# Layer 1 of a two-layer backbone: the output projection of the first eight heads beside the last head, for both halves of the columns

## The chip, the cores and the metric

The kernel runs on one core of one Trainium2 chip. The metric is the time of one execution on the device, in microseconds. Beside it there is one execution recorded by the hardware profiler, with its trace; that execution's own time stands in the table below.

Engines: PE multiplies matrices, PEld is its weight load, ACT, DVE and POOL work on SBUF and PSUM (the matmul accumulators), SP issues loads and POOL issues stores as DMA transfers. Each engine runs its instructions in the order of the built program; a waiting instruction holds all later ones of its engine.

## The reference, cut to what matters

The program computes two layers over 1024 latent tokens of width 1024 and 256 context tokens. Layer 1, the odd one, is a bidirectional gated linear recurrence of 16 heads, each with 128 value columns. What the change touches is its end, the product with `w_out`, the gate and the residual:

```python
def merge(o, z):
    o = _rms(jnp.swapaxes(o, 1, 2).astype(z.dtype), h_norm.reshape(HG_HEADS, HG_VDIM))
    return (o.reshape(o.shape[:2] + (HG_VW,)) * jax.nn.silu(z)) @ w_out
...
x = x + gate * y_lat
```

So out[1024, 1024] = x1 + gate * (y[1024, 2048] @ w_out[2048, 1024]), with y the normed and gated output of the 16 heads, 128 columns from each.

## The kernel before, in words

Everything is float32. For the matrix engine each operand is split in two parts, high and low: `split` (L72) casts the high part on ACT (L74) and subtracts it on DVE to get the low part (L75). A product then takes three matmuls for each block of 128 rows of the contraction: in `out_sum` yh by wh (L749), yh by wl (L750), yl by wh (L751), each 128 x 512.

Layer 1 is a loop over the 16 heads (`for h in range(16)`, in `build`). For each head: projections of the next head, scores inside chunks (`hg_intra`, the products named s and acc), the scan over states (`hg_scan`), then the norm and gate (squares on ACT at L1204 into gss, further steps on POOL and DVE, gz at L1208), and `hg_y`, which transposes gz on PE (tr, L1220), copies it (L1222, gyt) and stores the head's y by POOL's queue (L1223) to the DRAM array yd2 (printed yd) in two halves of 256 KB. The program is written in this order, but the tile framework's scheduler places each engine's instructions by priority and by when their inputs are there, so that matmuls of a later stage can stand between those of the last head.

The output projection is cut into 8 row tiles (tt, 128 tokens each), two halves of the columns (b = 1: columns 512 to 1023; b = 0: columns 0 to 511) and two halves of the contraction (q = 0: heads 0 to 7; q = 1: heads 8 to 15). One row tile for one b and one q is 8 blocks by 3 = 24 matmuls into one PSUM tile (mm). For it `out_y` (L730) reads y back from DRAM by SP (L736) in two halves of 256 KB into the raw buffers "wraw" of pool yp (3 of them), and splits each into yh and yl (2 buffers each). The weights for one b and q are 8 slabs of 128 x 512 (256 KB), loaded by SP (L103) into raw buffers and split into pairs of slab buffers (`wblock`, L80; its argument `ring` says for each slab which pool and how many buffers).

The stages before:

1. `out_ahead`, beside the last head (pool yp is opened when the normed input, hh and hl, is no longer needed, after the last projection, whose result gvT is copied at L1048): slabs of b = 1, q = 0 into a ring of 8 in yp ("wo"), raw in the heads' pool; 8 row tiles, each copied by ACT (L771) to SBUF (oacc). Then the slabs of b = 1, q = 1: four in pool wp ("w"), four in yp, raw in yp "woraw", 4 buffers.
2. Pool op1, b = 1: per row tile the product with q = 1, the row block of x1 (L782, oxh), then on DVE the addition of oacc (L786), the product with the gate (L788, og), the addition to x1 (L789), and the store of the result by POOL's queue (L1466). After each row tile two slabs of w1 are loaded and split: w1 holds all 16 slabs of b = 0 (`wo_half`, L726), with the four raw buffers "woraw".
3. b = 0: per row tile the product over q = 0 and q = 1 together (48 matmuls), no addition, gate and residual as above.

## Time and profile before

| | before |
|---|---|
| median of 3 runs | 3529.34 us (3528.73 to 3532.45) |
| the profiled execution's own time | 3531.36 us |
| its span in the trace | 3529.6 us |
| mean granted PE clock | 0.993 |
| PE busy | 3462.1 us, 24438 matmuls |

How to read it: the span runs from the first to the last instruction in the trace; the execution's own time is 1.8 us longer. PE is busy in 98% of the span. In the rows below, a line such as L749 is one of the kernel before; `mm<-woh,yh` means that mm is written from woh and yh, and an engine's idle time is put down to what released it last.

### The profile page before, as it was taken

The numbers are of one execution on the slowest core, as the hardware profiler recorded it, in microseconds if no ns is written. First come the engines' busy times: TensorE is split into PE (matmuls) and PEld (weight loads), VectorE is DVE, ScalarE is ACT, GpSimd is POOL, SyncE is SP. The second block draws the span as 40 slices with busy tenths as digits, with TensorE's granted clock in tenths as the row PEclk, the third lists the DMA queues.
The fourth block names the chain that finished last, engine by engine and source line by source line (L and its number), as shares of the span: only waits on it lengthen the run. The fifth ranks groups of instructions, "written<-read, shape, count | busy, mean of one in ns | idle before, by whom it ended". The sixth has DMA issues, their size and how long they took to land.

```text
span 3529.6 us, 64866 instructions
## 1 busy us (share of the span) xinstructions
PE 3462.1 (98%) x24438; PEld 3151.1 (89%) x24438; DVE 2370.4 (67%) x6001; ACT 1598.3 (45%) x3692; POOL 521.4 (15%) x836
## 2 busy tenths in 40 slices
PE   8999999999999999999999999999999999999988
PEld 5899999999999999987778999899999999999877
DVE  4669856766666654666677766577777777777852
ACT  5532135555444534555547323344444444444431
POOL 3211121222222211211211111001000000100010
PEclk9999999999999999999999999999999999999999
DMA  7542321322323225455483232212112111211353
GB/s 235 175 156 84 122 87 52 94 84 74 82 73 90 74 87 162 140 168 157 131 251 124 99 111 85 87 40 62 50 49 61 60 47 53 62 50 48 108 188 114
DMA packets 372618, 359.71 MB, mean 102 GB/s; under 512 B 30041, under 2 KB 322841, under 8 KB 372177
## 3 DMA queue, kind: packets, MB, share of 16 engines
q1 hardware_dynamic: 328944, 248.25, 23.9%
q0 software_dynamic: 43360, 107.32, 9.0%
q8 instruction: 193, 3.16, 0.4%
q14 instruction: 121, 0.98, 0.1%
HBM read 274.00 MB, written 81.32 MB: 101 GB/s over the span
## 4 chain that ended last, share of the span: by engine, by line
PE 83%; issue 8%; DMA 3%; DVE 2%; ACT 2%; POOL 1%; SPq 0%; POOLq 0%; DVEq 0%; ACTq 0%
PE mm L129 15%; PE mm L128 15%; PE mm L127 15%; PE s L1134 6%; PE acc L695 3%; PE tr L675 2%; PE sa L128 2%; PE sa L127 2%; PE sa L129 2%; PE acc L478 2%; PE s L485 2%; PE s L1179 1%; PE mm L749 1%; PE mm L750 1%; PE mm L751 1%
## 5 line engine op out<-in xcount | busy, mean ns | idle before, releaser
L127 PE MATMUL mm<-wh,hh 128*128 128x256 f32 x2256 | 648.8, 288 | 3.8 <-DVE ev L938 2.7
L128 PE MATMUL mm<-wl,hh 128*128 128x256 f32 x2256 | 648.8, 288 | 2.0 <-DVE wl L75 1.9
L129 PE MATMUL mm<-wh,hl 128*128 128x256 f32 x2256 | 648.4, 288 | 0.0
L129 PE MATMUL mm<-hh,wl 128*128 128x512 f32 (+1 forms) x1344 | 491.4, 366 | 0.0
L127 PE MATMUL mm<-hh,wh 128*128 128x512 f32 (+1 forms) x1344 | 485.2, 361 | 0.0
L128 PE MATMUL mm<-hl,wh 128*128 128x512 f32 (+1 forms) x1344 | 483.7, 360 | 0.0
L127 PEld LDWEIGHTS mm<-wh,hh 128*128 128x128 f32 x2256 | 431.1, 191 | 11.8 <-issue 6.9
L128 PEld LDWEIGHTS mm<-wl,hh 128*128 128x128 f32 x2256 | 431.4, 191 | 7.3 <-DVE wl L75 2.8
L129 PEld LDWEIGHTS mm<-wh,hl 128*128 128x128 f32 x2256 | 431.0, 191 | 3.6 <-issue 0.7
L74 ACT CAST wh<-wraw 128x512 fp32r<-128x512 f32 x282 | 173.4, 620 | 256.3 <-PE mm L128 125.7
L128 PEld LDWEIGHTS mm<-hl,wh 128*128 128x128 f32 x1344 | 254.0, 189 | 32.0
L129 PEld LDWEIGHTS mm<-hh,wl 128*128 128x128 f32 x1344 | 253.9, 189 | 30.5 <-issue 0.2
L127 PEld LDWEIGHTS mm<-hh,wh 128*128 128x128 f32 x1344 | 254.3, 189 | 29.3
L1125 ACT COPY gksel<-gK 128x512 f32<-128x512 f32 x224 | 147.0, 663 | 213.5 <-PE s L1134 204.4
L75 DVE TENSOR_TENSOR wl<-wraw,wh 128x512 fp32r<-128x512 f32 x282 | 191.2, 686 | 53.8 <-ACT wh L74 51.2
L1134 PE MATMUL s<-gQ,gksel 128*128 128x128 f32 x1536 | 199.8, 276 | 0.0
L1134 PEld LDWEIGHTS s<-gQ,gksel 128*128 128x128 f32 x1536 | 192.4, 191 | 7.0
L749 PE MATMUL mm<-woh,yh 128*128 128x512 f32 x444 | 180.4, 407 | 6.8 <-ACT yh L74 4.1
L751 PE MATMUL mm<-woh,yl 128*128 128x512 f32 x444 | 178.7, 403 | 0.7 <-DVE yl L75 0.5
L750 PE MATMUL mm<-wol,yh 128*128 128x512 f32 x444 | 177.8, 400 | 0.0
L1155 DVE TENSOR_TENSOR gQ<-gQ,gT 128x256 f32<-128x256 f32 x384 | 143.2, 414 | 28.1 <-PE s L1134 28.1
L74 ACT CAST wh<-b 128x512 fp32r<-128x512 f32 x124 | 77.0, 622 | 187.8 <-PE sa L129 79.5
(461 smaller groups left out, 8456.9 us busy)
## 6 DMA issues: line engine op xcount, KB each, us to landing
wraw<-yd SPq DMA_DIRECT2D x144, 256.0 KB
wraw<-in_wc_dram SPq DMA_DIRECT2D x128, 256.0 KB
wraw<-in_wab_dram SPq DMA_DIRECT2D x98, 256.0 KB
md<-ev POOLq DMA_DIRECT2D x94, 256.0 KB, 2.8
adar<-in_wada_dram POOLq DMA_DIRECT2D x32, 512.0 KB, 5.0
b<-in_wc_dram SPq DMA_DIRECT2D x64, 256.0 KB
vzd<-qo POOLq DMA_DIRECT2D x56, 256.0 KB, 2.5
adar<-in_wada_dram SPq DMA_DIRECT2D x16, 512.0 KB
```

What stands on the lines that cost most here:

```text
L74: nc.scalar.copy(hi, x)
L75: nc.vector.tensor_tensor(out=lo, in0=x, in1=hi.bitcast(F32), op=ALU.subtract)
L127: mm(ps, lhsT=lh(k), rhs=rh(k), start=(first and k == 0), stop=False)
L128: mm(ps, lhsT=lh(k), rhs=rl(k), start=False, stop=False)
L129: mm(ps, lhsT=ll(k), rhs=rh(k), start=False, stop=(last and k == nk - 1))
L695: m = nc.tensor.matmul(yp[h64], lhsT=v[:, h64], rhs=pTs[hd][:nk, i, :], start=(i == turn[0]), stop=(i == turn[-1]), tile_position=(0, hd * ...
L749: mm(ps, lhsT=yh[:, k, :], rhs=w.h(kk), start=(kk == 0), stop=False)
L750: mm(ps, lhsT=yh[:, k, :], rhs=w.l(kk), start=False, stop=False)
L751: mm(ps, lhsT=yl[:, k, :], rhs=w.h(kk), start=False, stop=(kk == 8 * len(qs) - 1))
L1125: nc.scalar.copy(ksel.rearrange("p (b s i) -> p b s i", s=2, i=h), pick(K))
L1134: nc.tensor.matmul(pa[:, c, :].rearrange("p (b s i) -> p b s i", s=2, i=h), lhsT=ksel[:, c * P : (c + 1) * P], rhs=qp[:, c * nbc : (c + 1) ...
L1155: nc.vector.tensor_tensor(out=t[:, i, :, s, :], in0=t[:, i, :, s, :], in1=bc(tot), op=ALU.mult)
```

## The change

Both halves of the columns are now computed for heads 0 to 7 (q = 0) beside the last head. The function `out_some`, which layer 0 uses already, does it: first for b = 1, with the sum kept in SBUF (oacc) as before, then for b = 0, where ACT copies the sum to a buffer ("ox", 2 of them) and POOL's queue stores it to a new DRAM array, `part`. For b = 0 the last stage then multiplies only q = 1 (24 matmuls a row tile), reads the part back by SP into a buffer of the op "og" (now 4 buffers, shared with the gate product) and adds it on DVE.

The slabs of the three blocks beside the last head (b = 1 q = 0, b = 0 q = 0, b = 1 q = 1) go through one list of 12 places: four in pool wp, eight in yp. The first block takes wp's four first, then yp; the third block takes only yp's eight. All three use the heads' pool for raws (3 buffers). The later slabs w1 are now 8 (b = 0, q = 1), in a pool of their own, and their raw buffers are yp's "wraw", 3 of them, the same that y is read into; two slabs are loaded after each of the first four row tiles of b = 1.

```diff
--- before.py
+++ after.py
@@ -723,10 +723,6 @@
         nc.gpsimd.dma_start(out=self.yd[p2], in_=z)
 
 
-    def wo_half(self, wsrc, rings, raw, later):
-        return self.wblock(None, "wo", [wsrc[:, 0:512]], 16, 512, raw, later=later, ring=rings)
-
-
     def out_y(self, tt, q, ysrc, yp, bufs, rp=None):
         yh = self.t(yp, [P, 8, P], F32R, "yh", bufs)
         yl = self.t(yp, [P, 8, P], F32R, "yl", bufs)
@@ -752,26 +748,14 @@
 
 
 
-    def out_some(self, w, q, order, ysrc, yp, acc):
+    def out_some(self, w, q, order, ysrc, yp, acc, dst):
         for tt in order:
             ps = self.ps("mm", [P, 512])
             self.out_sum(ps, w, tt, (q,), ysrc, yp, 2)
             o = self.t(yp, [P, 512], F32, "ox", 2) if acc is None else acc[:, tt, :]
             self.nc.scalar.copy(o, ps)
             if acc is None:
-                self.nc.gpsimd.dma_start(out=self.x1[tt * P : (tt + 1) * P, 0:512], in_=o)
-
-    def out_ahead(self, wsrc, nt, ysrc, yp, ring, rp=None):
-        acc = self.t(yp, [P, nt, 512], F32, "oacc", 1)
-        rows = lambda q: [wsrc[q * D : (q + 1) * D, 512:D]]
-        w = self.wblock(yp, "wo", rows(0), 8, 512, *((rp, 3, "wraw") if rp else (yp, 4, "woraw")), ring=ring)
-        for tt in range(nt):
-            ps = self.ps("mm", [P, 512])
-            self.out_sum(ps, w, tt, (0,), ysrc, yp, 2)
-            self.nc.scalar.copy(acc[:, tt, :], ps)
-        n = self.slabs if rp else 0
-        rings = [(self.wp, "w", n)] * n + [(yp, "wo", ring)] * (8 - n)
-        return acc, self.wblock(yp, "wo", rows(1), 8, 512, yp, 4, "woraw", ring=rings)
+                self.nc.gpsimd.dma_start(out=dst[tt * P : (tt + 1) * P, 0:512], in_=o)
 
 
     def out_tile(self, w, b, tt, ysrc, xsrc, xt, yp, op, bufs, ys=None, part=None):
@@ -1242,6 +1226,7 @@
             self.vzd = self.scratch(dr, "vzd", [2, LAT, 2 * D])
             self.md_all = self.scratch(dr, "md", [20, T, 256])
             self.md = {}
+            self.part = self.scratch(dr, "part", [LAT, 512])
 
             self.ident = self.t(cp, [P, P], F32, "ident")
             make_identity(nc, self.ident)
@@ -1363,7 +1348,7 @@
                             if g == ML_OUT[b][0]:
                                 wq[b] = wo(0, b)
                             for tt in [t for t, at_g in zip(ML_ORDER, ML_OUT[b]) if at_g == g]:
-                                self.out_some(wq[b], 0, [tt], self.yd, yp, acc if b else None)
+                                self.out_some(wq[b], 0, [tt], self.yd, yp, acc if b else None, self.x1)
                 w2 = wo(1, 1)
                 self.gate_bc(0, yp, 2, 1)
                 for tt in [8, 9, 3, 4, 2, 5, 1, 6, 0, 7]:
@@ -1449,20 +1434,30 @@
 
                 rh.close()
                 yp = es.enter_context(tc.tile_pool(name="oy", bufs=1, side="right"))
-                acc, w2 = self.out_ahead(a["woc"], 8, self.yd2, yp, 8, self.rawp)
-            self.ogb = 1
+                acc = self.t(yp, [P, 8, 512], F32, "oacc", 1)
+                ring = [(self.wp, "w", 4)] * 4 + [(yp, "wo", 8)] * 8
+                wo = lambda q, b, ring, raw, later=None: self.wblock(
+                    None, "wo", [a["woc"][q * D : (q + 1) * D, b * 512 : b * 512 + 512]], 8, 512, raw, later=later, ring=ring
+                )
+                raw = [pool, 3, "wraw"]
+                for i, b in enumerate((1, 0)):
+                    w = wo(0, b, (ring * 2)[8 * i : 8 * i + 8], raw)
+                    self.out_some(w, 0, range(8), self.yd2, yp, acc if b else None, self.part)
+                w2 = wo(1, 1, ring[4:], raw)
+            self.ogb = 4
             with tc.tile_pool(name="op1", bufs=2) as op, ExitStack() as wl:
                 later = []
                 wl1 = wl.enter_context(tc.tile_pool(name="wo1", bufs=1))
-                w1 = self.wo_half(a["woc"], [(wl1, "wo", 16)] * 16, [yp, 4, "woraw"], later)
+                w1 = wo(1, 0, [(wl1, "wo", 8)] * 8, [yp, 3, "wraw"], later)
                 for b, w in ((1, w2), (0, w1)):
                     self.gate_bc(1, op, 1, b)
                     for tt in range(8):
                         xt = self.t(op, [P, 512], F32, "oxh", 3)
-                        self.out_tile(
-                            w, b, tt, self.yd2, self.x1[tt * P : (tt + 1) * P], xt, yp, op, 2,
-                            part=acc[:, tt, :] if b else None,
-                        )
+                        part = acc[:, tt, :]
+                        if not b:
+                            part = self.t(op, [P, 512], F32, "og", 4)
+                            dma(out=part, in_=self.part[tt * P : (tt + 1) * P, :])
+                        self.out_tile(w, b, tt, self.yd2, self.x1[tt * P : (tt + 1) * P], xt, yp, op, 2, part=part)
                         nc.gpsimd.dma_start(out=a["out"][tt * P : (tt + 1) * P, b * 512 : (b + 1) * 512], in_=xt)
                         for ld in later[:2]:
                             ld()
```

Lines behind L764 of before have a number smaller by 16 in the changed kernel (L749 to L751 are L745 to L747, L736 is L732, L1208 is L1192, L1220 is L1204); the copies of L771 are at L756.

The scheduler decides the order on each engine. On PE, the end of the last head stood like this before (acc and tr belong to the last head, mm to the output projection of heads 8 to 15; numbers tell buffers apart):

```order
L1195 MATMUL acc_39323<-gv_39083,gA_38792 128x128
L1196 MATMUL acc_39323<-gS_7782_39256,gQ_38789 128x128
L1220 MATMUL tr_39360<-ident_73,gz_39085 128x128
L1197 MATMUL acc_39323<-gS_7810_39336,gQ_38789 128x128
L1195 MATMUL acc_39323<-gv_39083,gA_38792 128x128
L1196 MATMUL acc_39323<-gSc_7702_38932,gQ_38789 128x128
L1197 MATMUL acc_39323<-gS_7812_39343,gQ_38789 128x128
L1220 MATMUL tr_39368<-ident_73,gz_39085 128x128 x4
L749 MATMUL mm_39777<-woh_39742,yh_39778 128x512
```

and the same second half of the last head's transposes now, with the sums of b = 0, heads 0 to 7 (mm_39956 is the sixth row tile, mm_39994 the seventh):

```order
L746 MATMUL mm_39956<-wl_39754,yh_39957 128x512
L747 MATMUL mm_39956<-wh_39755,yl_39958 128x512
L1204 MATMUL tr_39369<-ident_74,gz_39086 128x128 x3
L745 MATMUL mm_39956<-wh_39761,yh_39957 128x512
L1204 MATMUL tr_39369<-ident_74,gz_39086 128x128
L746 MATMUL mm_39956<-wl_39760,yh_39957 128x512
L747 MATMUL mm_39956<-wh_39761,yl_39958 128x512
L745 MATMUL mm_39994<-woh_39719,yh_39995 128x512
```

The transposes stood between the last accumulations and the first matmul of heads 8 to 15, with nothing else beside them; now they stand among the matmuls of heads 0 to 7.

On SP, where the stage with b = 1, q = 1 begins, its loads before (wraw is y's ring, woraw the slabs' own; gbc is the gate, oxh the row blocks of x1):

```order
L736 DMA wraw_39780<-yd_4_66 128x4x128
L103 DMA woraw_39820<-in_woc_dram 128x512
L103 DMA woraw_39826<-in_woc_dram 128x512
L103 DMA woraw_39874<-in_woc_dram 128x512
L103 DMA woraw_39880<-in_woc_dram 128x512
L736 DMA wraw_39784<-yd_4_66 128x4x128
L736 DMA wraw_39834<-yd_4_66 128x4x128
L736 DMA wraw_39838<-yd_4_66 128x4x128
L736 DMA wraw_39888<-yd_4_66 128x4x128
L736 DMA wraw_39892<-yd_4_66 128x4x128
L736 DMA wraw_39942<-yd_4_66 128x4x128
L796 DMA gbc_39774<-gated_63 128x512
```

and now (the slab 40114 is the last of b = 1, q = 1 and has its raw in the heads' pool, 40173, 40179 and 40227 are slabs of w1):

```order
L732 DMA wraw_40133<-yd_4_66 128x4x128
L732 DMA wraw_40137<-yd_4_66 128x4x128
L103 DMA wraw_40173<-in_woc_dram 128x512
L103 DMA wraw_40179<-in_woc_dram 128x512
L732 DMA wraw_40187<-yd_4_66 128x4x128
L103 DMA wraw_40114<-in_woc_dram 128x512
L732 DMA wraw_40191<-yd_4_66 128x4x128
L780 DMA gbc_40127<-gated_63 128x512
L766 DMA oxh_40129<-x_7_69 128x512
L766 DMA oxh_40183<-x_7_69 128x512
L766 DMA oxh_40237<-x_7_69 128x512
L103 DMA wraw_40227<-in_woc_dram 128x512
```

Loads of y and of w1 now take turns in one ring of three buffers.

On ACT, around the copy gvT of the last projection, before (the casts of L74 are the first slabs of the output projection):

```order
L1204 ACTIVATE gjk_38650,gss_38649<-acc_38542 128x128 x2
L1144 COPY gA_38090<-s_38718 64x4x64
L1145 COPY gA_38090<-s_38718 64x4x64
L1204 ACTIVATE gjk_38650,gss_38649<-acc_38542 128x128
L1048 COPY gvT_38904<-mm_38879 128x256
L74 CAST woh_39382<-wraw_39383 128x512
L1204 ACTIVATE gjk_38650,gss_38649<-acc_38542 128x128
L74 CAST woh_39388<-wraw_39389 128x512
```

and now (wh are slabs in pool wp, woh slabs in yp):

```order
L74 CAST wh_39383<-wraw_39384 128x512
L74 CAST wh_39389<-wraw_39390 128x512
L808 ACTIVATE gq_38757<-mm_38732 128x512
L74 CAST wh_39395<-wraw_39396 128x512
L1109 COPY gksel_38717<-gK_38086 128x512
L1095 COPY gkn_38765<-tr_38760 128x512
L74 CAST wh_39401<-wraw_39402 128x512
L1032 COPY gvT_38905<-mm_38880 128x256
L74 CAST woh_39407<-wraw_39408 128x512
L74 CAST woh_39413<-wraw_39414 128x512
```

The casts of four slabs have moved ahead of the copy of gvT.

## The prediction

> **What bounds the kernel now.** I read the page first, for the span and for which engine is full.
>
> ```profile
> span 3529.6 us, 64866 instructions
> PE 3462.1 (98%) x24438; PEld 3151.1 (89%) x24438; DVE 2370.4 (67%) x6001; ACT 1598.3 (45%) x3692; POOL 521.4 (15%) x836
> ```
>
> PE is busy for 98% of the span, so a change that adds no matmul can only win what is left idle, or what PE runs at a low clock. The change begins at the last head, so I read the windows of the end of the run next (columns: window, its length, busy time and count of PE, PEld, DVE, ACT, POOL, granted PE clock, DMA share, GB/s).
>
> ```profile
> core 0: us, PE busy (x) PEld busy (x) DVE busy (x) ACT busy (x) POOL busy (x), PEclk, DMA share, GB/s
> 3279.00:3304.00 25.00, 20.22 (x111) 16.56 (x110) 22.64 (x51) 16.39 (x36) 2.63 (x4) 0.93 0.85 272
> 3304.00:3364.80 60.80, 60.80 (x371) 53.79 (x370) 41.89 (x103) 25.18 (x58) 4.04 (x6) 1.00 0.23 70
> 3364.80:3391.00 26.20, 17.53 (x89) 14.81 (x88) 8.54 (x21) 9.21 (x27) 3.66 (x6) 0.80 0.29 88
> 3391.00:3399.00 8.00, 8.00 (x37) 6.64 (x36) 4.62 (x9) 2.14 (x5) 0.54 (x1) 1.00 0.92 315
> 3399.00:3414.00 15.00, 12.92 (x55) 9.52 (x54) 13.34 (x22) 8.33 (x15) 1.08 (x2) 1.00 0.90 292
> 3414.00:3440.00 26.00, 26.00 (x115) 21.27 (x114) 15.14 (x25) 6.31 (x11) 2.70 (x5) 1.00 0.69 213
> 3440.00:3519.70 79.70, 79.70 (x341) 63.77 (x339) 26.06 (x41) 15.05 (x26) 3.79 (x7) 1.00 0.42 126
> ```
>
> PE has holes in three stretches: 4.78 us where the projection starts, 8.67 us at the end of the last head, and 2.08 us soon after it. Everywhere else it is full at full clock: the columns 0:512 run without a hole. The rate there, 79.70 / 341 = 0.234 us a matmul (0.230 between two starts below), makes a row tile of 24 matmuls 5.52 us. The timeline of PE names what each hole waited for (start, duration, and in brackets the idle time ahead and its releaser).
>
> ```profile
> 3282.73 1.12 PE L1064 MATMUL tr<-ident,gEc 128*128 128x128 f32 x4 [1.36 <-DVE gkn L1111]
> 3291.64 0.50 PE L749 MATMUL mm<-woh,yh 128*128 128x512 f32 x1 [0.92 <-ACT woh L74]
> 3296.30 0.50 PE L749 MATMUL mm<-woh,yh 128*128 128x512 f32 x1 [0.28 <-ACT yh L74]
> 3302.01 0.74 PE L749 MATMUL mm<-woh,yh 128*128 128x512 f32 x2 [1.76 <-ACT woh L74]
> 3371.58 0.99 PE L1220 MATMUL tr<-ident,gz 128*128 128x128 f32 x3 [3.02 <-DVE gz L1208]
> 3380.15 1.01 PE L1220 MATMUL tr<-ident,gz 128*128 128x128 f32 x4 [3.62 <-DVE gz L1208]
> 3383.20 0.79 PE L749 MATMUL mm<-woh,yh 128*128 128x512 f32 x1 [2.03 <-ACT yh L74]
> 3387.20 0.63 PE L749 MATMUL mm<-woh,yh 128*128 128x512 f32 x1
> 3387.63 0.63 PE L750 MATMUL mm<-wol,yh 128*128 128x512 f32 x1
> 3390.07 0.40 PE L750 MATMUL mm<-wl,yh 128*128 128x512 f32 x1
> 3390.30 0.39 PE L751 MATMUL mm<-wh,yl 128*128 128x512 f32 x1
> 3400.28 0.47 PE L749 MATMUL mm<-wh,yh 128*128 128x512 f32 x1 [0.74 <-DVE oacc L786]
> 3412.50 0.47 PE L749 MATMUL mm<-wh,yh 128*128 128x512 f32 x1 [0.93 <-DVE oacc L786]
> 3413.61 0.50 PE L751 MATMUL mm<-wh,yl 128*128 128x512 f32 x1 [0.41 <-DVE yl L75]
> ```
>
> The 8.67 us are 3.02 + 3.62 + 2.03: the norm and gate of the last head, twice, and the last head's y on its way through DRAM. Around them the clock falls: matmuls start every 0.43 us at 3387.20, every 0.23 us at 3390.07. The chain of waits shows what the first of these holes holds (start, length, engine):
>
> ```profile
> 3367.86 0.24 PE acc L1197 x2
> 3370.11 1.04 POOL gss L154
> ```
>
> From the last accumulation (3368.10) to the transpose of gz (3371.58) it is 3.48 us.
>
> **The change, part by part.** 768 output matmuls, 64 halves of y and 32 slabs stay as they are in number. What moves is 8 row tiles of 24 matmuls (columns 0:512, heads 0 to 7), from the full stretch after 3414 to beside the last head.
>
> *A. The start.* Its hole holds 0.92 + 0.28 + 1.76 = 2.96 us of late slabs and y. The new ring puts the first four slabs into buffers that are free before the last projection ends, and ACT's order has their casts ahead of gvT. I take -2.5; bounds 0 (the 0.85 DMA share stays, so slabs may land no sooner) and -4.8 (the whole hole).
>
> *B. The serial end.* Its 8.67 us of holes now meet 8 x 5.52 = 44 us of matmuls that depend on nothing in the last head: PE's order has them between the accumulations and the transposes, about one row tile, 5.5 us, against the 3.48 us chain. The half clock goes with the holes: the window's clock is 0.80, so between 0.20 x 17.53 = 3.5 us (loss shared evenly with the idle time) and 0.20 x 26.2 = 5.2 us (all of it in busy time); middle 4.4. B = -8.67 - 4.4 = **-13.1**, bounds -9 (clock still low) and -14. What is late next is the last head's y. Its transposes now stand in the sixth of the eight tiles, so two tiles, 11.0 us, are left for transpose, write, read and split:
>
> ```profile
> 3384.03 3.67 DMA yd<-gyt
> 3389.70 7.12 DMA woraw<-in_woc_dram
> 3405.05 6.07 DMA woraw<-in_woc_dram
> 3425.77 4.25 DMA wraw<-yd
> ```
>
> 1 + 3.67 + 4.25 + 1.5 = 10.4 us, just inside.
>
> *C.* The waits at 3400.28, 3412.50 and 3413.61 (2.08 us) belong to the stage that D makes anew: -2.1, bounds 0 and -2.1.
>
> *D. The new ring.* This is the cost. Before, the later slabs (w1) had four raw buffers of their own and y had three. Now one ring of three carries both, so during the first four tiles of columns 512:1024 each tile draws four raws (two of y, two slabs) through three buffers. SP issues a load only when the split that held the buffer is done, and behind a load that waits SP holds every later one. A buffer's round is the latency L plus the hold, from the cast and subtraction:
>
> ```profile
> L74 ACT CAST yh<-wraw 128x512 fp32r<-128x512 f32 x64 | 37.9, 619 | 96.5 <-PE mm L750 68.9 <-DMA wraw<-yd 24.2 <-DVE oacc L786 3.0
> L75 DVE TENSOR_TENSOR yl<-wraw,yh 128x512 fp32r<-128x512 f32 x64 | 43.0, 686 | 40.6 <-ACT yh L74 40.5
> L786 DVE TENSOR_TENSOR oacc<-mm,oacc 128x512 f32<-128x512 f32 x8 | 5.5, 683 | 0.6 <-PE mm L751 0.6
> L771 ACT COPY oacc<-mm 128x512 f32<-128x512 f32 x8 | 4.6, 581 | 2.2 <-PE mm L751 2.2
> ```
>
> 0.62 + 0.69 + about 0.2 of hand-offs (my allowance) = 1.5 us. A tile then takes 4/3 x (L + 1.5), if that is over 5.52. The head start is small: ahead of the first two slabs ACT and DVE split the last four slabs of heads 8 to 15, whose buffers come free in the last tile beside the head. L is the open price. The trace has it from 7.12 and 6.07 us (0.9 DMA share) over 4.25 (0.69 share) down to this load, issued at 3306.90 and cast 2.87 us later (0.23 share):
>
> ```profile
> 3306.90 2.84 SPq L736 DMA_DIRECT2D wraw<-yd  x3
> 3309.77 0.63 ACT L74 CAST yh<-wraw 128x512 fp32r<-128x512 f32 x1 [0.57 <-DMA wraw<-yd]
> ```
>
> In the new stage a tile moves four raws, a row block of x1 and one of out: 6 x 256 KB in 7.6 us, 207 GB/s, nearest to the 213 GB/s of the 0.69 window. So L = 4.25: 4/3 x 5.75 = 7.67, +2.15 a tile, **+8.6** over four. Bounds: L = 2.87 gives 5.83 and +1.2; L = 7.12 gives 11.5 and +23.9.
>
> On L the Trainium skill, "DMA: Bandwidth & Descriptors", section "Anatomy of one DMA — SWDGE (gpsimd) path", has a fit for one transfer of about 2.0 us plus bytes / 436 GB/s, an estimate of 2.6 us for 256 KB; by it a tile would take 5.5 us and D would be nothing. The nearest row, 2.87 us, is close to it, the loaded rows are not.
>
> After a stall of some 2 us the clock may fall too, as around the hole of 1.36 us at 3282.73:
>
> ```profile
> 3280.00:3285.00 5.00, 3.19 (x14) 2.67 (x15) 5.00 (x12) 4.63 (x13) 1.47 (x2) 0.76 0.89 237
> ```
>
> 1.81 us idle in all, and a clock of 0.76. I add nothing: while the ring sets the pace, PE has time in hand.
>
> The Trainium skill, "TensorE: Matmul & The Clock Gate", section "Why this matters for your kernels", asks only that no gap is over about 3 us; by it stalls of 2 us cost no clock and the sum stays as it is. The 0.76 beside a gap of 1.36 us speaks against it.
>
> *E. The tail and the copies.* The run's end gains one addition, since columns 0:512 now have a part:
>
> ```profile
> 3519.33 0.40 PE L751 MATMUL mm<-woh,yl 128*128 128x512 f32 x1
> 3519.77 0.69 DVE L788 TENSOR_TENSOR og<-mm,gbc 128x512 f32<-128x512 f32 x1 [8.76 <-PE mm L751]
> 3521.48 0.54 POOL L1466 DMA_DIRECT2D out_dram<-oxh  x1 [10.23 <-DVE oxh L789]
> ```
>
> +0.7 (the L786 row, 0.683). The other 7 additions, 8 copies on ACT (0.58 each, the L771 row; 4.6 us if nothing covered them), 8 writes of 256 KB on POOL's queue and 8 reads on SP's lie beside matmuls: ACT is busy 25.18 of 60.80 us beside the last head, DVE 26.06 of 79.70 beside columns 0:512. In program order the parts are written some 80 us before they are read. Bounds 0 and, if a wait for a part held each tile by one addition, 8 x 0.69 = 5.5.
>
> **Sum**: -2.5 - 13.1 - 2.1 + 8.6 + 0.7 = -8.4. The profiled execution took 3531.36 us (1.8 around its span), so 3523.0; it lies 2.0 above the median of 3529.34, so against that **3520.9 us**.
>
> **The rivals.** *The ring is hidden.* L is 2.87 as under light load: only three loads can be in flight now, where seven could be, and the two stretches with 0.9 DMA share held such a burst. D = +1.2, sum -15.8, **3513.5**. Against it: 4.25 in a stretch that was less crowded than those.
>
> *The ring costs more.* L of 5 to 6 gives 8.7 to 10 a tile, D = +13 to +18, sum -4 to +1: **3525 to 3530**. For it: 6.07 us at 3405.05, in the very stage.
>
> *The fill doesn't cover.* The order is right but the last head's y comes late, or the clock stays low: half of B is left, +6.5: **3527.4**. For it: 10.4 us against 11.0 is thin.
>
> *Slower: the ring of three at loaded latency.* Place: the first four tiles of columns 512:1024. Price: at L = 7.12, +23.9, and a tile with y alone takes 2/3 x 8.62 = 5.75, +0.23 x 12 = 2.8 over the other tiles; sum -8.4 - 8.6 + 26.7 = +9.7, **3539.0**. It turns slower than before from D = 17, that is L = 5.8, and measurably slower from D = 24, L = 7.2 (7.0 with the later tiles). Against it: 7.12 was met with more loads in flight.
>
> **How the numbers follow.** About 0.2% (7 us) is what a measurement of this kernel can tell from no change: under 3522.3 is faster, over 3536.4 slower. Chances: forecast (D of 5 to 12, 3517 to 3524.5) 0.50; ring hidden 0.20; ring costs more 0.12; fill doesn't cover 0.10; slower 0.08. Of the forecast, the part with L under 4.5 (D under 9.9) is faster, 0.38 of the 0.50. Faster: 0.20 + 0.38 = 0.58. Same: 0.12 + 0.12 + 0.10 = 0.34. Slower: 0.08. The range goes from the hidden ring to the dear one: 3513.0 to 3530.0; the slower case and the outer ends of the others, under 2 in 10, are left out.
>
> **What would show it.** A: no wait for a slab ahead of the first output matmuls. B: no wait for gz, full clock through the last head's end, and the first tile of heads 8 to 15 not waiting for its y. D: SP waiting for splits, PE waiting for yh in tiles 1 to 4 of columns 512:1024, some 2 us each, 7.7 us from tile to tile, and none later; four loads at about 4.2 us. E: three operations of DVE behind the last matmul. I am wrong if tiles in D run at 5.5 us or over 9, or if gz still stops PE.

## The result: 0.56% faster, below the forecast range

| | before | changed |
|---|---|---|
| median | 3531.9 us (6 runs, 3528.73 to 3534.21) | 3511.01 us (6 runs, 3508.98 to 3516.22) |
| ratio | | 0.9944, 95% interval 0.9931 to 0.9957 |
| profiled execution / its span | 3531.36 / 3529.6 us | 3510.13 / 3508.3 us |
| mean granted PE clock | 0.993 | 0.995 |

The forecast was 3520.9 us, the range 3513.0 to 3530.0. The sign was right; the gain is some 20 us instead of 8.4.

The spans of profiled executions cannot be subtracted blindly: PE's instructions are the same in both kernels up to about 3270 us, yet one and the same instruction well ahead of that falls between 2988.5 and 3001.8 us in the kernels of this study. So I measure a **stretch**: from one pair of instructions of DVE, gz, in the common part, to the end of the span. The timeline of DVE, before and then changed:

```profile
2994.17 0.60 DVE L1208 SCALAR_TENSOR_TENSOR gz<-acc,gss,gz 128x128 f32<-128x128 f32 x2
```

```profile
2993.07 0.60 DVE L1192 SCALAR_TENSOR_TENSOR gz<-acc,gss,gz 128x128 f32<-128x128 f32 x2
```

The stretch is 3529.6 - 2994.2 = 535.4 us before and 3508.3 - 2993.1 = 515.3 changed: **-20.1 us**, and only 1.1 us of the spans' difference lies ahead of it. Each kernel below has its stretch from its own trace, one execution each.

The windows of the end of the changed kernel (columns as in the prediction):

```profile
core 0: us, PE busy (x) PEld busy (x) DVE busy (x) ACT busy (x) POOL busy (x), PEclk, DMA share, GB/s
3278.00:3304.00 26.00, 24.82 (x141) 21.39 (x140) 22.65 (x54) 17.66 (x38) 2.85 (x4) 1.00 0.75 233
3304.00:3364.00 60.00, 60.00 (x370) 53.22 (x369) 44.16 (x106) 27.02 (x61) 4.43 (x7) 1.00 0.37 113
3364.00:3405.00 41.00, 41.00 (x216) 34.94 (x215) 13.82 (x29) 15.52 (x39) 6.90 (x12) 1.00 0.42 132
3405.20:3440.70 35.50, 30.21 (x122) 23.02 (x120) 20.24 (x31) 12.07 (x20) 2.70 (x5) 0.95 0.67 204
3440.70:3502.20 61.50, 61.45 (x265) 49.49 (x263) 33.48 (x54) 12.32 (x20) 5.94 (x11) 1.00 0.67 209
```

The last head's end (3364 to 3405) is full at full clock. The start has one hole of 1.18 us and full clock, where before there were 4.8 us and a clock of 0.93. All that is left is 5.3 us of holes in 3405 to 3441, the stage that takes the ring of three. The timeline of PE has every hole of the changed kernel, with the last head's transposes and a slow matmul between them:

```profile
3279.85 0.50 PE L745 MATMUL mm<-wh,yh 128*128 128x512 f32 x1 [1.18 <-ACT yh L74]
...
3393.16 0.49 PE L1204 MATMUL tr<-ident,gz 128*128 128x128 f32 x3
3393.73 0.27 PE L1204 MATMUL tr<-ident,gz 128*128 128x128 f32 x1
...
3419.48 0.79 PE L745 MATMUL mm<-woh,yh 128*128 128x512 f32 x1 [3.23 <-ACT yh L74]
3420.07 0.63 PE L746 MATMUL mm<-wol,yh 128*128 128x512 f32 x1
...
3428.13 0.50 PE L745 MATMUL mm<-woh,yh 128*128 128x512 f32 x1 [1.36 <-ACT yh L74]
...
3434.85 0.50 PE L745 MATMUL mm<-woh,yh 128*128 128x512 f32 x1 [0.69 <-ACT yh L74]
```

No transpose waits for gz any more. PE waits for yh three times, ahead of the third, fourth and fifth tile of columns 512:1024; behind the first of these the matmuls run at half rate (0.63 us) for 3.4 us. From first matmul to first matmul the second to fifth tile take 8.83, 8.65, 6.72 and 5.84 us, the others of that stage 5.44: the stage loses 8.3 us, about what D forecast (8.6), but not in four equal parts. SP's timeline shows why the first is the worst:

```profile
3408.06 0.33 SPq L780 DMA_DIRECT2D gbc<-gated  x1
3408.44 1.49 SPq L766 DMA_DIRECT2D oxh<-x  x3
3410.03 0.90 SPq L103 DMA_DIRECT2D wraw<-in_woc_dram  x2
3411.77 7.20 SPq L732 DMA_DIRECT2D wraw<-yd  x2
```

and ACT's who waited:

```profile
3417.23 1.38 ACT L74 CAST woh<-wraw 128x512 fp32r<-128x512 f32 x2 [6.21 <-DMA wraw<-in_woc_dram]
3418.81 0.62 ACT L74 CAST yh<-wraw 128x512 fp32r<-128x512 f32 x1 [0.20 <-DMA wraw<-yd]
...
3427.46 0.62 ACT L74 CAST yh<-wraw 128x512 fp32r<-128x512 f32 x1 [1.94 <-DMA wraw<-yd]
```

Seven loads start within 3.7 us (gate, three row blocks of x1, two slabs, a half of y). The slab issued at 3410.03 is cast at 3417.23, 7.2 us later, and the next half of y can be issued only at 3418.6, when a raw buffer is free. (The last row, the cast that PE's second wait ends with, is used below.)

The second surprise is behind the last matmul. By the windows of the two kernels it was 9.9 us to the end before, and it is 6.1 now, although one addition was added:

```profile
3502.20:3508.30 6.10, 0.00 (x0) 0.00 (x0) 2.06 (x3) 0.00 (x0) 0.54 (x1) 0.70 0.22 86
```

The instructions that close the program have a line of their own. POOL's drain among them (count; shortest / median / longest in ns; first and last start), before and then changed:

```profile
L1603 POOLq DRAIN  x3: 46/98/7335, 3521.5 to 3529.3; - x3
```

```profile
L1598 POOLq DRAIN  x3: 46/98/2939, 3504.6 to 3508.1; - x3
```

The first drain took 7.34 us before and 2.94 now: 4.4 us. The prediction has no term for it.

### The profile page after: what moved, and what is told of

Its sections match the earlier page's. It is cut to its first block, busy times and chain, and to the rows that moved or that the text cites. A ratio compares the mean times of both kernels' runs of the same rounds, so it can differ in the third digit from the quotient of the medians.

```text
span 3508.3 us, 64938 instructions
## 1 busy us (share of the span) xinstructions
PE 3453.9 (98%) x24438; PEld 3146.4 (90%) x24438; DVE 2374.5 (68%) x6009; ACT 1602.3 (46%) x3700; POOL 526.2 (15%) x844
## 5 line engine op out<-in xcount | busy, mean ns | idle before, releaser
L74 ACT CAST wh<-wraw 128x512 fp32r<-128x512 f32 x290 | 178.2, 620 | 263.1 <-PE mm L128 130.7
L745 PE MATMUL mm<-woh,yh 128*128 128x512 f32 x412 | 166.7, 405 | 6.7 <-ACT yh L74 6.5
L747 PE MATMUL mm<-woh,yl 128*128 128x512 f32 x412 | 165.3, 402 | 0.5 <-DVE yl L75 0.5
L746 PE MATMUL mm<-wol,yh 128*128 128x512 f32 x412 | 164.0, 399 | 0.0
L74 ACT CAST wh<-b 128x512 fp32r<-128x512 f32 x124 | 77.0, 622 | 187.1 <-PE sa L129 85.3
```

The lines of the kernel that those rows point to most:

```text
L74: nc.scalar.copy(hi, x)
L745: mm(ps, lhsT=yh[:, k, :], rhs=w.h(kk), start=(kk == 0), stop=False)
L746: mm(ps, lhsT=yh[:, k, :], rhs=w.l(kk), start=False, stop=False)
L747: mm(ps, lhsT=yl[:, k, :], rhs=w.h(kk), start=False, stop=(kk == 8 * len(qs) - 1))
```

## The experiments

**Theory R:** the stalls of part D come from the ring of three that y and the late slabs share. **Theory T:** they come from the traffic, whatever ring. First the ring is undone (`e1_own_raws`):

```diff
-                w1 = wo(1, 0, [(wl1, "wo", 8)] * 8, [yp, 3, "wraw"], later)
+                w1 = wo(1, 0, [(wl1, "wo", 8)] * 8, [yp, 3, "woraw"], later)
```

> The changed kernel, but the later slabs (w1) have three raw buffers of their own again, so y keeps its three. Theory R (the ring of three shared by y and w1 makes the stalls of the first tiles of columns 512:1024): the three waits of PE for yh (3.23, 1.36, 0.69 us) and the half-clock window after the first go, tiles 2 to 5 of that stage take 5.44 us instead of 8.8, 8.7, 6.7, 5.9: about -8 us, near 3503. Theory T (the burst of seven loads at the start of the stage, each over 6 us to landing, makes the first stall whichever ring): the first stall of about 3 us and its half clock stay, only the later ones go: -2 to -4 us, near 3508.

Median 3504.27 us, ratio to before 0.9928 (0.9913 to 0.9943), stretch 507.7: -7.6 against the changed kernel. The window of its columns 512:1024:

```profile
3405.00:3450.00 45.00, 45.00 (x201) 37.25 (x200) 28.85 (x47) 15.42 (x27) 4.32 (x8) 1.00 0.76 232
```

No hole at a DMA share of 0.76, more than the 0.67 of the changed kernel's stalling stage. R holds; traffic of this size alone stops nobody here.

The same ring with four buffers for both (`e3_ring_of_four`; in layer 1 alone):

```diff
-            yr = self.t(rp or yp, [P, 512], F32, "wraw", 3).rearrange("p (j t) -> p j t", j=4)
+            yr = self.t(rp or yp, [P, 512], F32, "wraw", self.yb).rearrange("p (j t) -> p j t", j=4)
...
+                self.yb = 4
...
-                w1 = wo(1, 0, [(wl1, "wo", 8)] * 8, [yp, 3, "wraw"], later)
+                w1 = wo(1, 0, [(wl1, "wo", 8)] * 8, [yp, self.yb, "wraw"], later)
```

> The changed kernel, but the ring that y and w1 share has four raw buffers instead of three. Theory R: a tile draws four raws through four buffers, one round, 5.7 us: about -6 us, near 3505; the waits for yh fall under 0.5 us each. Theory T: one more load may join the burst; the first stall stays, -2 to -4 us.

Median 3506.29, ratio 0.9934 (0.9919 to 0.9949), stretch 511.3: -4.0. Two stalls remain (1.73 and 0.99 us), so the closed form (one round, 5.7 us) was too kind; it has the mean latency and not the burst's, which is the likely reason.

The slabs spread out, one a tile (`e2_one_slab_a_tile`):

```diff
-                        for ld in later[:2]:
+                        for ld in later[:1]:
                             ld()
-                        later = later[2:]
+                        later = later[1:]
```

> The changed kernel, but one slab of w1 after each of the eight tiles of columns 512:1024 instead of two after each of the first four. A tile then draws three raws through three buffers: one round, L + 1.5. Theory R: at the 4.2 us of the later loads 5.7 us a tile, so at most 0.3 us a tile over PE's 5.44: about -6 us, near 3505. Theory T: the burst loses one load of seven, the first stall stays at 2 to 3 us: -2 to -4, near 3508.

Both were wrong. Median 3514.04, ratio 0.9949 (0.9933 to 0.9966), stretch 516.6: +1.3. The first three tiles run at 5.4 to 5.6 us, the stalls come later and go on in columns 0:512, where no slab is loaded (5.8 to 7.5 us a tile). Its waits of SP there, 3460 to 3505 (us in all, times, longest):

```profile
SPq L766 <- DMA out_dram<-oxh: 30.6, 8, 4.7
```

SP waits at the loads of x1 until a result is stored, since x1's three buffers are also the results'. In the changed kernel it waits as long (29.7 us from 3450 to 3500) and it costs nothing, because y is a tile ahead there. Here the lead is lost when the stage begins, y stands behind those waits in SP's queue, and the lead does not come back. The read of the part stands there too: three of PE's four holes in that stretch are put down to the addition of the part (og L770), which in all waits 16.9 us for that read and holds one of the two accumulators (mm) meanwhile. In the changed kernel these additions wait as long (16.3 us) and PE is not stopped. To test this, six buffers for x1 (`e11_one_slab_six_x1`; beside the edit above):

```diff
-                        xt = self.t(op, [P, 512], F32, "oxh", 3)
+                        xt = self.t(op, [P, 512], F32, "oxh", 6)
```

> One slab of w1 a tile, as in the kernel e2_one_slab_a_tile, and six buffers for x1 (oxh) instead of three. In that kernel the tiles of columns 0:512 took 5.8 to 7.6 us, and SP waited 30.6 us for stores at the loads of x1, with the loads of y queued behind. Theory: those waits kept y late; with six buffers SP does not wait for stores, y gets ahead again, and the kernel comes to about 3506 (8 us under that one by the trace's own stretch). Rival: the ring of three with three raws a tile is the cause itself, and the tiles stay over 5.7 us.

Median 3507.68, ratio 0.9939 (0.9924 to 0.9954), stretch 513.3: -3.2 against one slab a tile, and less than half of the forecast; tiles of columns 0:512 still take 5.6 to 6.8 us. Half right: SP's waits for stores fell (17.7 us from 3450 to 3495, its own trace), and others, for part's buffers and for splits, took their place; the additions wait 4.0 us for the part instead of 16.9.

Then the burst. The slabs start behind the third tile instead of the first, so two tiles later in spite of the name (`e9_slabs_one_tile_later`):

```diff
-                        for ld in later[:2]:
-                            ld()
-                        later = later[2:]
+                        if tt > 1 or not b:
+                            for ld in later[:2]:
+                                ld()
+                            later = later[2:]
```

> The changed kernel, but the slabs of w1 start behind the third tile of columns 512:1024 instead of the first (two a tile, four tiles). Two theories of the first stall (3.23 us and a half-clock window): burst (two slabs of w1 land 7 us late because seven loads, of the gate, x1 and the slabs, start within 4 us, and y waits behind them in the ring): with no slab in the ring then, the first stall goes, and the four tiles with slabs, at 4.2 us a load, lose about 2 us each at most later: some -2 to -4 us against the changed kernel. Ring alone (four raws through three buffers, whenever they come): the same loss of 8 us, only later: no change.

Median 3510.29, ratio 0.9938 (0.9921 to 0.9955), stretch 514.1: -1.2. Its windows of the first five tiles (with the end of the tile ahead of them), the next three with the first of columns 0:512, and the other seven:

```profile
3405.00:3436.00 31.00, 31.00 (x137) 25.35 (x135) 17.76 (x29) 11.47 (x20) 2.71 (x5) 1.00 0.72 224
3436.00:3460.00 24.00, 22.93 (x97) 17.91 (x97) 16.68 (x26) 6.89 (x13) 2.17 (x4) 1.00 0.70 218
3460.00:3504.00 44.00, 41.57 (x168) 32.14 (x167) 20.82 (x33) 7.43 (x12) 3.87 (x8) 0.96 0.64 202
```

The first stall is gone with the slabs taken out of the burst, and the tiles with slabs lose 1.07 us of holes (2.2 us by their lengths), with four raws a tile through three buffers as before: the ring at 4.2 us a load is not what made most of the changed kernel's loss. The start of the stage did; whether by the burst's latency or because y gets no lead when slabs enter the ring at once is not told apart, since this edit changes both. What was won is lost in columns 0:512, by 4.9 us over the fourth to seventh tile, again with y and the part late:

```profile
3477.54 0.47 PE L745 MATMUL mm<-woh,yh 128*128 128x512 f32 x1 [0.50 <-DVE og L770]
3491.31 0.47 PE L745 MATMUL mm<-woh,yh 128*128 128x512 f32 x1 [1.89 <-DVE og L770]
```

```profile
DVE og L770 <- DMA og<-part: 18.4, 6, 4.1
```

**Part A.** Its list turned, so that wp's four places come last (`e4_wp_slabs_last`):

```diff
-                ring = [(self.wp, "w", 4)] * 4 + [(yp, "wo", 8)] * 8
+                ring = [(yp, "wo", 8)] * 8 + [(self.wp, "w", 4)] * 4
```

> The changed kernel, but the list of slab places is turned, so that the first block takes the eight places in yp and wp's four come later: part A of the change is undone. If A is what the earlier slabs give, the holes ahead of the first output matmuls come back (PE waiting for woh, about 3 us and a half-clock window): +3 to +5 us, near 3515. Rival: the fuller order alone covers them and nothing changes (3511).

Median 3516.92, ratio 0.9963 (0.9948 to 0.9978), stretch 520.2: +4.9, of which 4.2 lie ahead of the first tile of heads 8 to 15. The holes of 0.30, 0.17 and 1.36 us come back, and one of 1.05 us at an output matmul; the half clock does not (the clock is 1.00 from 3275 to 3305). And A alone, put into the kernel before (`e6_ring_alone_on_before`):

```diff
-        w = self.wblock(yp, "wo", rows(0), 8, 512, *((rp, 3, "wraw") if rp else (yp, 4, "woraw")), ring=ring)
+        first = [(self.wp, "w", 4)] * 4 + [(yp, "wo", ring)] * 4
+        w = self.wblock(yp, "wo", rows(0), 8, 512, *((rp, 3, "wraw") if rp else (yp, 4, "woraw")), ring=first)
...
-        rings = [(self.wp, "w", n)] * n + [(yp, "wo", ring)] * (8 - n)
+        rings = [(yp, "wo", ring)] * 8
```

> The kernel before with one part of the change: the first block's slabs go to wp's four places first, then yp; the second block takes yp's eight. Part A by itself: the holes at the start (0.92, 0.28, 1.76, 1.36 us) and the half-clock window among them go, -4 to -5 us against before, near 3526; the holes of 3.02, 3.62 and 2.03 us at the last head stay. Rival: A needs the fuller order, and nothing changes (3530).

Median 3523.45 (10 runs) against 3530.11 (19 runs), ratio 0.9983 (0.9972 to 0.9993), that is 2 to 10 us; stretch 525.5: -9.9, from the fastest of its ten executions, so near the upper end. Its timeline of PE has these holes and no others behind 3270:

```profile
3279.50 0.50 PE L749 MATMUL mm<-wh,yh 128*128 128x512 f32 x1 [1.18 <-ACT yh L74]
...
3364.18 0.84 PE L1221 MATMUL tr<-ident,gz 128*128 128x128 f32 x3 [3.06 <-DVE gz L1209]
...
3371.53 1.10 PE L1221 MATMUL tr<-ident,gz 128*128 128x128 f32 x4 [3.52 <-DVE gz L1209]
...
3375.06 0.80 PE L749 MATMUL mm<-woh,yh 128*128 128x512 f32 x1 [2.42 <-ACT yh L74]
```

All of the start's holes are one of 1.18 us, and the three waits of part C are gone too. The last head's three stand, as expected. By the first matmuls of its tiles, 6.8 of the 9.9 us lie ahead of the second tile of heads 8 to 15 and 3.1 in that stage's other seven. Not all of the 6.8 belong to the start: at the last head this execution has half clock for 6.8 us, the one of before for 10.2.

**Part B**, by leaving the fill out (`e5_no_fill`):

```diff
-                    self.out_some(w, 0, range(8), self.yd2, yp, acc if b else None, self.part)
+                    if b:
+                        self.out_some(w, 0, range(8), self.yd2, yp, acc, self.part)
+                for tt in range(8):
+                    nc.gpsimd.dma_start(out=self.part[tt * P : (tt + 1) * P, :], in_=acc[:, tt, :])
```

> The changed kernel without the eight row tiles of columns 0:512, heads 0 to 7 (192 matmuls, their y loads, splits and copies are left out; the sums of the other half are stored to part in their place, so columns 0:512 of the output lack their part). The tiles are worth 8 x 5.44 = 43.5 us of PE. Theory: they fill the waits of the last head, so without them the holes for gz and for the last head's y come back with their half clock, some 13 us: 3511 - 43.5 + 13 = 3480.5. Rival: the waits went for another reason (the order of the slabs, the earlier start) and don't come back: 3467.5.

Median 3482.93, ratio 0.9865 (0.9847 to 0.9883), stretch 486.6: -28.7 for 43.5 us of matmuls less. So 14.8 us came back. It is no pure size of B: the last head's end lost 16.4 us, the stage with the ring lost 2.4 less than in the changed kernel, and the rest 0.9 more. Its timeline of PE has the holes back:

```profile
3367.70 0.96 PE L1204 MATMUL tr<-ident,gz 128*128 128x128 f32 x3 [3.06 <-DVE gz L1192]
3376.58 1.25 PE L1204 MATMUL tr<-ident,gz 128*128 128x128 f32 x4 [3.53 <-DVE gz L1192]
3379.45 0.79 PE L745 MATMUL mm<-woh,yh 128*128 128x512 f32 x1 [1.63 <-ACT yh L74]
```

3.06 + 3.53 + 1.63 = 8.22 us against the 8.67 of the kernel before; two smaller ones (0.75 and 0.45 us) stand ahead of them, and three waits for y (1.91, 1.21, 0.39) behind.

**The closing drain.** First theory: it is long where POOL had idled (10.2 us ahead of the last store before, 2.7 after). The kernel before with its stores in halves (`e7_stores_in_halves`):

```diff
-                        nc.gpsimd.dma_start(out=a["out"][tt * P : (tt + 1) * P, b * 512 : (b + 1) * 512], in_=xt)
+                        for c in (0, 256):
+                            nc.gpsimd.dma_start(
+                                out=a["out"][tt * P : (tt + 1) * P, b * 512 + c : b * 512 + c + 256], in_=xt[:, c : c + 256]
+                            )
```

> The kernel before, but each result row block is stored in two halves of 256 columns, one right behind the other. At the end POOL's closing drain took 7.34 us in the kernel before and 2.94 in every kernel with the change. Theory: it is long where POOL had idled some 10 us ahead of its last store (10.2 before, 2.7 after), so with a second store right behind the first it is short: the end comes 4.4 us sooner, less some 0.5 for the second store. Rival: the drain's length hangs on something else (the program, the place): 7.3 us again, and the same time as before.

The drain took 3.08 us, from the last matmul to the end it was 6.0 instead of 9.9, and the stretch 532.2 (-3.2). Median 3528.97 (10 runs), ratio 0.9988 (0.9978 to 0.9999). It looked like the theory. The opposite test, idling made in the changed kernel (`e10_pool_idle_at_end`):

```diff
-                        nc.gpsimd.dma_start(out=a["out"][tt * P : (tt + 1) * P, b * 512 : (b + 1) * 512], in_=xt)
+                        (nc.gpsimd if b or tt not in (5, 6) else nc.scalar).dma_start(
+                            out=a["out"][tt * P : (tt + 1) * P, b * 512 : (b + 1) * 512], in_=xt
+                        )
```

> The changed kernel, but the stores of the sixth and seventh tile of columns 0:512 are issued by ACT instead of POOL, so that POOL idles some 15 us ahead of its last store. If POOL's idle time sets the closing drain, it takes 7.3 us instead of 2.9, and the span ends some 3.7 us later (about 3515). Rival: the drain depends on something else, and nothing changes beyond 1 us.

```profile
L1600 POOLq DRAIN  x3: 46/98/2855, 3509.2 to 3512.5; - x3
```

Median 3512.41, ratio 0.9952 (0.9937 to 0.9966), stretch 515.4. POOL idled 12.1 us and the drain is short: the theory falls. What was left in common was the number of POOL's stores in the whole program (POOL issues 486 transfers in the kernel before, 494 in the changed one, 502 and 492 in these two). Eight were taken from the changed kernel (`e13_part_stored_by_act`) and eight given to the kernel before (`e14_before_eight_more_stores`):

```diff
-                self.nc.gpsimd.dma_start(out=dst[tt * P : (tt + 1) * P, 0:512], in_=o)
+                eng = self.nc.scalar if dst is self.part else self.nc.gpsimd
+                eng.dma_start(out=dst[tt * P : (tt + 1) * P, 0:512], in_=o)
```

> The changed kernel, but the eight stores to part are issued by ACT instead of POOL, so that POOL issues as many stores as in the kernel before. If the number of POOL's stores over the program sets the closing drain, it takes 7.3 us again and the end comes 4 us later (about 3515). Rival: the drain hangs on the last stage (a store every 5.6 us instead of 11.2), and stays 2.9 us (3511).

```diff
             self.nc.scalar.copy(acc[:, tt, :], ps)
+            self.nc.gpsimd.dma_start(out=self.part[tt * P : (tt + 1) * P, :], in_=acc[:, tt, :])
```

> The kernel before with eight more stores on POOL's queue: the sums of columns 512:1024, heads 0 to 7, are also stored to a DRAM array that nothing reads. If the number of POOL's stores sets the closing drain, it falls from 7.3 to 2.9 us and the kernel gains 4 us (near 3527), though it does more. Rival: the last stage sets it, 7.3 us stay, and the time is that of before or a little more.

The drains, of the first and then of the second:

```profile
L1599 POOLq DRAIN  x3: 46/98/7335, 3503.0 to 3510.9; - x3
```

```profile
L1605 POOLq DRAIN  x3: 46/97/2937, 3516.5 to 3520.0; - x3
```

The number decides, in both directions: with as many stores as before the changed kernel has a drain of 7.34 us, stretch 518.6 (+3.4; the stage with the ring lost 1.0 less in this execution), median 3514.39, ratio 0.9950 (0.9935 to 0.9965); with eight more the kernel before has 2.94, stretch 529.8 (-5.7, of which 4.4 behind the last matmul), median 3526.23 (10 runs), ratio 0.9984 (0.9975 to 0.9994). Why a number of stores does this stays open.

**Two further kernels.** The late slabs in other places (`e8_late_slabs_elsewhere`; four are loaded behind the first two tiles of columns 512:1024 and four behind its last):

```diff
-                w1 = wo(1, 0, [(wl1, "wo", 8)] * 8, [yp, 3, "wraw"], later)
+                w1 = wo(1, 0, ring[:8], [yp, 3, "woraw"], later)
...
-                        for ld in later[:2]:
+                        if tt == 7:
+                            for ld in later:
+                                ld()
+                            later = []
+                        for ld in later[:2] if tt < 2 else []:
                             ld()
-                        later = later[2:]
+                        later = later[2:] if tt < 2 else later
```

> The changed kernel, but the slabs of w1 go to the places in wp (four, loaded behind the first two tiles of columns 512:1024) and yp (four, loaded behind its last tile), with three raw buffers of their own. In the last stage matmuls started every 0.234 us, in the stage ahead every 0.227. Theory: the pace hangs on where the slabs lie; with places of the faster stage the last 192 matmuls take 0.227 each, -1.4 us against the kernel with raws of its own, 3503 if the four late slabs come in time. Rival: the pace belongs to the stage, and 0.234 stays; four late slabs may stop PE for 1 to 3 us at its start.

Matmuls of the last stage start every 0.227 us instead of 0.234 (median of the last 190). Median 3502.88, ratio 0.9917 (0.9897 to 0.9936), stretch 506.9, 0.8 under e1_own_raws. Same stage, same y, other slab buffers: the pace goes with where the slabs lie. The change itself has this effect too: it moves eight tiles of columns 0:512 from slabs of the slow kind (5.62 us a tile before) to places in wp and yp (5.44 a full tile).

One operation less behind the last matmul (`e12_own_raws_short_tail`):

```diff
-        if part is not None:
+        if part is not None and not b and self.ogb == 4:
+            nc.vector.tensor_tensor(out=part, in0=part, in1=self.gbc[:, v, :], op=ALU.mult)
+            nc.vector.tensor_tensor(out=xt, in0=xt, in1=part, op=ALU.add)
+        elif part is not None:
```

> The changed kernel with raws of their own for w1 (as e1_own_raws) and, in columns 0:512, the part multiplied with the gate and added to x1 ahead of the last matmul, so that two operations of DVE follow it instead of three. Expected: e1's time less one operation of 0.69 us, near 3503.5, under both kernels. Rival: the fourth operation a tile delays DVE's splits and eats it.

Median 3505.62, ratio 0.9928 (0.9914 to 0.9943), stretch 508.8, +1.1 against e1. The tail is shorter (5.7 us), but 1.08 us of waits for yh and yl appear where columns 0:512 begin: nothing won. Best of all is e8; e1, with one word changed, lies 1.4 us above it, which these runs can't tell apart.

## Why the prediction was wrong, step by step

The two traces can be compared stretch by stretch, cut at the first matmuls of output tiles. The seven tiles behind the first of heads 8 to 15, and then columns 0:512 up to the last matmul, take before:

```profile
3388.45:3429.61 41.16, 39.08 (x170) 31.13 (x168) 30.59 (x49) 16.68 (x30) 3.24 (x6) 1.00 0.83 263
3429.61:3519.33 89.72, 89.72 (x384) 72.13 (x383) 31.05 (x49) 17.70 (x31) 4.87 (x9) 1.00 0.45 135
```

and in the changed kernel, where columns 0:512 have eight tiles fewer:

```profile
3410.65:3457.02 46.37, 41.08 (x170) 32.04 (x168) 26.94 (x42) 12.71 (x22) 3.78 (x7) 0.96 0.71 213
3457.02:3502.15 45.13, 45.13 (x193) 35.97 (x191) 24.10 (x38) 8.67 (x14) 4.32 (x8) 1.00 0.66 209
```

Seven full tiles are 38.1 us, so the stage lost 3.1 us before and loses 8.3 now. Ahead of it, A and B together won 20.2 us (the eight new tiles taken off at 5.44 us each): 5.3 of them are the start (3.6 of holes and 1.7 of half clock), the rest B.

| part | forecast | by the two traces | by an experiment |
|---|---|---|---|
| A, start | -2.5 | -5.3 | -4.2 ahead of the ring's stage (e4 undoes it) |
| B, serial end | -13.1 | -14.9 | -13.4 (changed against e6), -16.4 (e5) |
| C, later waits | -2.1 | -3.1 | -3.1 (e6) |
| D, ring of three | +8.6 | +8.3 | +7.6 (e1) |
| pace of the eight tiles moved | none | -1.5 | (e8 shows the pace) |
| E, the end | +0.7 | -3.7 | drain -4.4 (e13, e14) |
| sum | -8.4 | -20.2; the stretches differ by -20.1 | |

Each size comes from one execution. The sum closes because it is the same two traces cut up; between executions a part moves by a window or two of half clock. B has three sizes for that reason: at the last head, half clock lasted 6.8 us in e6, 10.2 in the kernel before and 13.7 in e5.

By these traces the forecast change is 11.8 us short. The largest misses are E, 4.4 us, and A, 2.8; B, C and the pace make the rest, and D's error is small.

**The step that failed first is A.** The prediction took -2.5 and set -4.8, the holes alone, as the furthest it could go. It counted the waits for slabs and y and took the hole of 1.36 us, with the half clock beside it, as staying. But the first slabs are not only less late: they are there before the last projection ends, so that PE has output matmuls to put into that hole, and neither the hole nor its half-clock window is left. The trace had the price of the window (clock 0.93 over 25 us, 1.7 us), and I had charged the clock in B and not in A. That price is not a fixed one: e4 and e7 have the same three holes, 0.30, 0.17 and 1.36 us, at full clock; the last section has the difference.

**C came true for another reason.** Its waits are gone in e6 already, which leaves that stage's raw buffers as they were and only gives its slabs other places.

**A term was put at nothing: the pace.** The prediction began from the sentence that a change without new matmuls can only win idle time or low clock, and took one tile time, 5.52 us, for all. A tile takes 5.62 us in columns 0:512 and 5.44 elsewhere, so eight tiles gained 1.5 us by their move.

**E failed in sign.** The tail was worked out up to the last store. The 8.1 us from its issue (3521.48) to the end of the span were in the trace and were taken as given. 4.4 of them hung on the number of POOL's stores, which the change raised by eight. This could not have been forecast from the profile of before; that the tail was unexplained could.

**B was right** in mechanism and nearly in size: 8.67 us of holes and 4.2 of half clock make 12.9, and some 2 us more are tiles that ran long without a hole. The last head's y, just inside by my count (10.4 of 11.0 us), stopped nobody: no hole stands at the first tile of heads 8 to 15.

**D was right in sum and half wrong in form,** so the agreement of the sums is in part luck. The place, the queue and the ring are confirmed by e1. But the middle latency of 4.25 us in four like tiles was not what happened: the start of the stage, with over 7 us on its first loads, made most of it, and the later tiles lost 1.3 and 0.4. The rival with a hidden ring gave 3513.5, nearest to the measured time, for a reason that did not hold. The half clock behind a stall, to which I gave nothing, came after the hole of 3.23 us and slowed 3.23 us of busy time, 1.6 us of loss. It was covered, as "PE has time in hand" says: the next hole, 1.36 us, ends with a cast (3427.46) that waited for its load and not for PE, so at full clock PE would have come 1.6 us sooner and waited that much longer.

## What to carry to other kernels

Price a hole with the half-clock window beside it and ask whether the change brings work that is ready for it; here A and C gave 8.4 us where the waits named in the forecast came to 2.96 + 2.08. Follow the chain to the end of the span, not to the last store: the largest miss lay in 8.1 us that nothing explained. Look for what fills the buffers when a stage opens: its first loads start together, and a ring that is shared with a late stream can take their latency, not the mean. Here a lead of one tile hid 29.7 us of waits in SP's in-order queue, and the two kernels that lost it (e2, e9) did not regain it within the stage.

## What the runs showed of the hardware

- POOL's closing drain took 7.34 us or 2.9 to 3.1 us, by the number of transfers issued on POOL's queue in the program: 7.34 with 486 (before, e6, e13), 2.86 with 492 (e10), 2.94 with 494 (the changed kernel, e14), 3.08 with 502 (e7, sixteen half stores more). POOL's idle time ahead of it did not matter (e10). Other numbers were not tried, so this is no rule for more or fewer.
- Matmuls of the same shape started every 0.227 or every 0.234 us, 3%, over whole stages. Moving the slabs to other buffers changed it (e8); what about the place does it was not tried.
- In all 16 traces, behind the first 200 us, the granted clock changes only on a grid of 3.413 us that runs on through the program. Of the grid's windows at full clock, none of the 3281 in which PE idled less than 0.4 was followed by half clock, 26 of the 62 with 0.4 to 0.6 were, and all 61 with 0.6 or more were. So what a hole costs in clock hangs on how it falls on the grid: the same three holes fill 0.49 of a window in the kernel before, with half clock behind it, and 0.40 of one in e4, with none.
- The same instruction in the part that is common to all kernels came between 2988.5 and 3001.8 us. Over the 16 kernels, the distance of the profiled execution from its kernel's median (-5.7 to +6.8 us) follows this time with a correlation of 0.97: most of the scatter of these times arises ahead of the change.
